# TensorE in written order through the whole program

## The chip, the core and the metric

The kernel runs on one core of a Trainium2 chip. The metric is the time of one execution in device microseconds; lower is better. TensorE (PE in the profile) does the matmuls and the transposes, VectorE (DVE) and ScalarE (ACT) the elementwise work, GpSimd (POOL) issues the indirect gathers, and SyncE (SP) the loads of the weights.

## The reference

A transformer-like net on 256 tokens of width 2048, in float32:

```python
# block 1
h = rmsnorm(x, g_norm1); proj = h @ w_in
y_a = mla_branch(proj, ...) @ w_o_mla        # latent attention, 8 heads, rope on 64 of 192 columns
y_b = diff_branch(proj, ...) @ w_o_diff      # softmax(q1 k1) - lam * softmax(q2 k2), 8 heads
gates = sigmoid(proj[..., OFF_GATE:] + b_gate)
x = x + (gates[..., :D] * y_a + gates[..., D:] * y_b) @ w_out
# peer: per token, 8 heads x 16 experts out of 16384, found by two top-16 searches
q = (h @ w_q).reshape(t, 8, 2, 128); s1, s2 = q . sub_keys
experts, gates = top16(top16(s1) + top16(s2))
a = gelu(sum_d expert_u[experts] * h)
x = x + sum_k (gates * a)[k] * expert_v[experts[k]];  x = rmsnorm(x, g_final)
# even mixer: 4 retention heads of 256 and a gated convolution of width 3, then w_out
x = x + even_mixer(rms_norm(x), ev_w_in, ev_conv_w, ev_w_out)
# odd mixer: 32 query heads on 4 key heads, a window of 128, sinks, a silu gate, then w_out
x = x + odd_mixer(rms_norm(x), od_w_in, ..., od_w_out)
```

## The kernel before

Every projection goes through `dense` (lines 158 to 186). A weight block of 512 columns (w_kr: 320) is loaded in parts of two k rows (line 106, SP); `prep` splits each part into a high half (ACT, line 109) and a low half (DVE, line 110), up to three parts ahead, in four buffers `hl`. PE then runs, for each k and each of the two token tiles (t0, t1), three matmuls into one PSUM bank: x_hi·w_hi (line 177), x_hi·w_lo (178), x_lo·w_hi (179). These are called dense matmuls below; the program has 6156 of them. The stages are block 1 (w_ckvq, w_kr, w_ukv, w_uq, w_dqkv, w_gate, then w_oa/w_ob, w_out), w_qp with the routing, the row stream, the even mixer (ev_in, ev_out) and the odd mixer (od_in, od_out).

After each part `dense` calls `tick`. When a block of columns is done, its two evacuations (`ev_...`, one for each t) are started as generators: each does its ACT and DVE work on the bank, yields a number of ticks, and then issues its transposes (`transpose4`, line 206) or score matmuls, which need the result of that work. Attention units (`mla_unit`, lines 471 to 482; `diff_unit`, 524 to 551; retention and the odd mixer's attention, 1115 to 1169) run as such generators between the parts too. `settle`, in the last k part of a projection's first block, and `flush`, called after some projections, tick until what is open is done; there all the rest is issued at once.

PSUM has four banks for `acc`, two for `tr` (transposes) and two for `sd` (scores and attention outputs).

In the row stream 256 groups of 128 gathered rows of expert_u and 256 of expert_v (128x2048 each) arrive by indirect DMA (line 773) in a few slots; DVE makes a dot product of each u group (line 799) and PE multiplies each v group (line 815). The first u gathers are issued, and their dots made, while w_qp still runs: `route` finds the experts of a block of heads (DVE, lines 653 to 703), writes them as `ef`, and `spread` transposes `ef` on PE (line 664).

What sets the order: the program is recorded through a tile framework whose scheduler orders the instructions of each engine by its own estimate of when their inputs are there. Only inside `with self.tc.manual_schedule(engines={PE, Pool})`, which before stands around the row stream's loop alone (line 846), do the named engines keep the order in which the code issues. DVE, ACT and POOL elsewhere, and PE elsewhere, are ordered by the scheduler.

Of the kernel before, what the change touches and what calls it, by code (L numbers as in the profile page):

```python
# [42 lines left out]
class Builder:  # L43
# [258 lines left out]
    def build(self):  # L302
        nc, d = self.nc, self.d
        for w in ("w_ckvq", "w_kr", "w_ukv", "w_uq", "w_dqkv", "w_gate", "w_oa", "w_out1", "w_qp"):
            if w == "w_oa":
                wa, wb = d["w_oa"], d["w_ob"]
                for b in range(4):
                    for ww in (wa, wb):
                        self.add_plan(ww[b:b + 1])
            else:  # L310
                self.add_plan(d[w])
        self.limit = len(self.plan)
        for w in ("ev_in", "ev_out", "od_in", "od_out"):
            self.add_plan(d[w])
        cst = self.cst
        self.mhalf = cst.tile([P, 8], F32, tag="mhalf", name="mhalf")
        nc.gpsimd.memset(self.mhalf, -0.5)
        self.ident = cst.tile([P, P], F32, tag="ident", name="ident")
        make_identity(nc, self.ident)
        wz = cst.tile([P, 512], F16, tag="wz", name="wz")  # L320
        nc.vector.memset(wz, 0.0)
        wp = self.sd()
        for _ in range(14):
            nc.tensor.matmul(wp, wz[:, :P], wz, start=True, stop=True)
        self.block1()
        self.peer()
        self.even()
        self.odd()

    def stat_sum(self, ss4, tag):  # L330
        out = self.cst.tile([P, 2], F32, tag=tag + "_ss", name=tag + "_ss")
# [954 lines left out]
```

## Time and profile before

| | |
|---|---|
| median of three runs | 2896.06 us (2892.47, 2896.06, 2896.06) |
| profiled execution | 2892.76 us, span 2891.0 us |
| PE busy | 2330.3 us, 81% |
| DVE busy | 1687.0 us, 58% |
| ACT busy | 790.2 us, 27% |
| POOL busy | 669.1 us, 23% |
| moved by DMA | 820.24 MB, 284 GB/s over the span |
| mean granted clock of PE | 0.898 |

The span runs from the first to the last instruction of the profiled execution; its time is a little longer. A share of busy time is a mean over stages with different limits, so the rows are read by stage. A number in brackets in a timeline row is the idle time of the engine ahead of it, and what ended it.

### The profile page before, as it was taken

How to read it: one execution, taken by the hardware profiler on the slowest of the kernel's cores; microseconds unless marked ns; L12 is line 12 of the kernel's file. 1: busy time of each engine (PE TensorE's matmuls, PEld its weight loads, DVE VectorE, ACT ScalarE, POOL GpSimd, SP SyncE). 2: the span in 40 equal slices, each digit the busy share in tenths (PEclk: the TensorE clock that was granted, in tenths of full speed). 3: DMA queues.
4: the chain of work that ended last, by engine and by line, in shares of the span. 5: the costliest groups of instructions: out<-in, count | busy, mean ns of one | idle time of the engine just before them, and what ended most of it. 6: DMA issues, size and time to landing. Idle time of an engine off the chain costs nothing.

```text
span 2891.0 us, 26312 instructions
## 1 busy us (share of the span) xinstructions
PE 2330.3 (81%) x9488; PEld 1460.5 (51%) x9488; DVE 1687.0 (58%) x2503; ACT 790.2 (27%) x1244; POOL 669.1 (23%) x570
## 2 busy tenths in 40 slices
PE   9999999999515656665666565667899999999999
PEld 7878888888401111111111111111488888888887
DVE  5665755667999554444455444441464556677754
ACT  6544644444200000000000000000344444456653
POOL 0000000000354564444445454533100000000000
PEclk9999999999857877778787868789999999999999
DMA  7545466556989999999999999999755455553345
GB/s 253 170 144 183 156 217 200 186 187 208 360 319 363 408 421 420 420 420 420 420 420 420 420 420 420 420 420 420 278 182 191 160 181 185 191 173 132 124 152 169
DMA packets 151955, 820.24 MB, mean 284 GB/s; under 512 B 17232, under 2 KB 17264, under 8 KB 85776
## 3 DMA queue, kind: packets, MB, share of 16 engines
q0 software_dynamic: 75360, 543.75, 46.0%
q1 hardware_dynamic: 76464, 274.81, 28.5%
q8 instruction: 74, 1.21, 0.2%
q14 instruction: 57, 0.47, 0.0%
HBM read 816.39 MB, written 2.10 MB: 283 GB/s over the span
## 4 chain that ended last, share of the span: by engine, by line
PE 52%; DMA 19%; issue 15%; POOL 8%; DVE 6%; ACT 0%; SPq 0%; POOLq 0%; ACTq 0%; DVEq 0%
PE acc L177 15%; PE acc L178 15%; PE acc L179 15%; DMA hg<-expert_v,eidv 7%; DMA gslot<-expert_v,eidv 7%; POOL gslot L773 4%; POOL hg L773 3%; DMA hj<-expert_v,eidv 2%; DVE hj L799 2%; PE tr L206 2%; PE acc L815 1%; DMA gslot<-expert_u,eidx 1%; PE sd L1115 1%; POOL hj L773 1%; PE sd L1124 1%
## 5 line engine op out<-in xcount | busy, mean ns | idle before, releaser
L110 DVE TENSOR_TENSOR hl<-raw,hl 128x1024 fp32r<-128x1024 f32 (+1 forms) x516 | 623.3, 1211 | 529.1 <-ACT hl L109 528.7
L109 ACT ACTIVATE hl<-raw 128x1024 fp32r<-128x1024 f32 (+1 forms) x516 | 541.2, 1049 | 766.8 <-PE acc L179 612.1
L177 PE MATMUL acc<-hl,h 128*128 128x512 f32 (+1 forms) x1472 | 582.4, 396 | 2.6 <-ACT hl L109 2.6
L178 PE MATMUL acc<-hl,h 128*128 128x512 f32 (+1 forms) x1472 | 573.8, 390 | 4.8 <-DVE hl L110 4.8
L815 PE MATMUL acc<-hg,lw 128*32 128x512 f32 x880 | 415.5, 823 | 199.7 <-DMA hg<-expert_v,eidv 195.8
L179 PE MATMUL acc<-hl,h 128*128 128x512 f32 (+1 forms) x1472 | 573.8, 390 | 0.0
L815 PE MATMUL acc<-gslot,lw 128*32 128x512 f32 x848 | 422.8, 820 | 174.0 <-DMA gslot<-expert_v,eidv 173.8
L799 DVE CUSTOM_DVE_ANT_0 hj<-gslot,hj 128x2048 f16<-128x2048 f32 x121 | 277.0, 2289 | 238.2 <-DMA gslot<-expert_u,eidx 238.1
L799 DVE CUSTOM_DVE_ANT_0 hj<-hg,hj 128x2048 f16<-128x2048 f32 x116 | 265.5, 2289 | 207.9 <-DMA hg<-expert_u,eidx 207.5
L177 PEld LDWEIGHTS acc<-hl,h 128*128 128x128 f32 x1472 | 277.6, 189 | 64.8 <-issue 6.6
L178 PEld LDWEIGHTS acc<-hl,h 128*128 128x128 f32 x1472 | 277.7, 189 | 61.5 <-DVE hl L110 7.2
L179 PEld LDWEIGHTS acc<-hl,h 128*128 128x128 f32 x1472 | 277.3, 188 | 57.6 <-issue 0.3
L815 PEld LDWEIGHTS acc<-hg,lw 128*32 128x32 f32 x880 | 81.1, 141 | 441.7 <-DMA hg<-expert_v,eidv 273.8
L815 PE MATMUL acc<-hj,lw 128*32 128x512 f32 x320 | 214.4, 825 | 88.1 <-DMA hj<-expert_v,eidv 88.1
L815 PEld LDWEIGHTS acc<-gslot,lw 128*32 128x32 f32 x848 | 81.7, 140 | 397.1 <-DMA gslot<-expert_v,eidv 252.4
L786 ACT ACTIVATE dots<-dots 128x32 f32<-128x32 f32 x8 | 1.8, 229 | 988.3 <-DVE dots L799 988.3
L194 POOL TENSOR_TENSOR rs_y<-rs_v,mhalf 128x2 f32<-128x2 f32 (+2 forms) x25 | 28.0, 1121 | 804.2 <-DVE rs_v L193 803.5
L773 POOL DMA_INDIRECT hg<-expert_v,eidv x110 | 147.6, 1342 | 181.6 <-PE acc L815 137.3
L773 POOL DMA_INDIRECT gslot<-expert_v,eidv x106 | 135.0, 1274 | 205.2 <-PE acc L815 164.8
L773 POOL DMA_INDIRECT gslot<-expert_u,eidx x121 | 129.2, 1068 | 179.4 <-issue 70.4
L773 POOL DMA_INDIRECT hg<-expert_u,eidx x116 | 139.7, 1204 | 118.9 <-issue 26.8
L815 PEld LDWEIGHTS acc<-hj,lw 128*32 128x32 f32 x320 | 40.8, 142 | 199.1 <-DMA hj<-expert_v,eidv 119.0
(303 smaller groups left out, 2393.8 us busy)
## 6 DMA issues: line engine op xcount, KB each, us to landing
raw<-ev_in SPq DMA_DIRECT2D x128, 512.0 KB, 4.5
raw<-od_in SPq DMA_DIRECT2D x72, 512.0 KB, 3.9
raw<-w_gate SPq DMA_DIRECT2D x64, 512.0 KB, 4.3
raw<-w_dqkv SPq DMA_DIRECT2D x48, 512.0 KB, 3.5
raw<-w_out SPq DMA_DIRECT2D x32, 512.0 KB, 3.9
raw<-w_qp SPq DMA_DIRECT2D x32, 512.0 KB, 4.4
raw<-ev_out SPq DMA_DIRECT2D x32, 512.0 KB, 4.6
raw<-od_out SPq DMA_DIRECT2D x32, 512.0 KB, 4.5
```

What stands on the lines that cost most here:

```text
L109: nc.scalar.activation(hi, raw, AF.Copy)
L110: nc.vector.tensor_tensor(lo, raw, hi.bitcast(F32), op=ALU.subtract)
L177: nc.tensor.matmul(o, xh, wh, start=(k == 0), stop=False)
L178: nc.tensor.matmul(o, xh, wl, start=False, stop=False)
L179: nc.tensor.matmul(o, xl, wh, start=False, stop=(k == kc * kk - 1))
L194: nc.gpsimd.tensor_tensor(y, v, self.mhalf[:, :n], op=ALU.pow)
L206: self.nc.tensor.transpose(ps[:, j * P:(j + 1) * P], row[:, j * P:(j + 1) * P], self.ident)
L773: nc.gpsimd.indirect_dma_start(out=g[0], out_offset=None, in_=d[table], in_offset=bass.IndirectOffsetOnAxis(ap=ix, axis=0))
L799: nc.vector.tensor_tensor_reduce(junk, g[0], hrow[:, t], 1.0, 0.0, op0=ALU.mult, op1=ALU.add, accum_out=dots[:, t, k:k + 1])
L815: nc.tensor.matmul(st["acc"][n][32 * q:32 * q + 32], lws[t, b][:, q, i], g[0][:, n * 512:(n + 1) * 512], start=(x % P < 4), stop=(x % P >= ...
L1115: nc.tensor.matmul(ps[:, i * W:(i + 1) * W], qT[hf, h // 2, q], kT[hf, g, :W], start=True, stop=True)
L1124: nc.tensor.matmul(po[:, i * 64:(i + 1) * 64], pT[:, i * (t + 1) + k], vo[:, k, g * 64:(g + 1) * 64], start=(k == 0), stop=(k == t))
```

## The change

The four stages are issued inside a `manual_schedule` for PE alone, so that PE's rows stand everywhere in the order in which the code issues them. The other engines are still ordered by the scheduler, whose rows move a little with PE's. The line numbers after 326 grow by one.

```diff
@@ -322,10 +322,11 @@
         wp = self.sd()
         for _ in range(14):
             nc.tensor.matmul(wp, wz[:, :P], wz, start=True, stop=True)
-        self.block1()
-        self.peer()
-        self.even()
-        self.odd()
+        with self.tc.manual_schedule(engines={mybir.EngineType.PE}):
+            self.block1()
+            self.peer()
+            self.even()
+            self.odd()
```

The first place is the end of w_kr on PE (`cl` are the latents that w_ukv multiplies, `ev` the rows that `ev_kr` made, `tr` the banks of transposes). Before, from the 7th dense matmul of w_ukv on:

```order
L177 MATMUL acc_717<-hl_624,cl_229 128x512
L178 MATMUL acc_717<-hl_624,cl_229 128x512
L206 MATMUL tr_726<-ident_84,ev_685 128x128 x2
L179 MATMUL acc_717<-hl_624,cl_229 128x512
L177 MATMUL acc_718<-hl_624,cl_229 128x512
L178 MATMUL acc_718<-hl_624,cl_229 128x512
L179 MATMUL acc_718<-hl_624,cl_229 128x512
L177 MATMUL acc_717<-hl_641,cl_229 128x512
L206 MATMUL tr_733<-ident_84,ev_677 128x128
L178 MATMUL acc_717<-hl_641,cl_229 128x512
L179 MATMUL acc_717<-hl_641,cl_229 128x512
L177 MATMUL acc_718<-hl_641,cl_229 128x512
```

And now, at the same place on PE (buffer numbers differ by a few):

```order
L178 MATMUL acc_520<-hl_609,h1_116 128x320
L179 MATMUL acc_520<-hl_609,h1_116 128x320
L206 MATMUL tr_721<-ident_84,ev_675 128x128 x2
L206 MATMUL tr_728<-ident_84,ev_687 128x128 x2
L206 MATMUL tr_735<-ident_84,ev_679 128x128
L206 MATMUL tr_738<-ident_84,ev_691 128x128
L177 MATMUL acc_719<-hl_626,cl_231 128x512
L178 MATMUL acc_719<-hl_626,cl_231 128x512
```

Of the four sets of transposes that stood behind the 1st, 8th, 13th and 16th dense matmul of w_ukv (the second and the third are in the rows of before) all now stand ahead of the first.

The second place is the end of ev_in on PE, where `flush` stands (`eT` is what ev_out multiplies). Before, from the 11th dense matmul of ev_out on:

```order
L178 MATMUL acc_11066<-hl_10988,eT_8399 128x512
L206 MATMUL tr_11047<-ident_84,ev_10895 128x128 x4
L179 MATMUL acc_11066<-hl_10988,eT_8399 128x512
L177 MATMUL acc_11065<-hl_11005,eT_8399 128x512
L178 MATMUL acc_11065<-hl_11005,eT_8399 128x512
L179 MATMUL acc_11065<-hl_11005,eT_8399 128x512
L177 MATMUL acc_11066<-hl_11005,eT_8399 128x512
L178 MATMUL acc_11066<-hl_11005,eT_8399 128x512
L179 MATMUL acc_11066<-hl_11005,eT_8399 128x512
L177 MATMUL acc_11065<-hl_11005,eT_8399 128x512
L206 MATMUL tr_11055<-ident_84,ev_10897 128x128 x4
```

And now there:

```order
L178 MATMUL acc_10902<-hl_10973,h3_7372 128x512
L179 MATMUL acc_10902<-hl_10973,h3_7372 128x512
L206 MATMUL tr_11049<-ident_84,ev_10897 128x128 x4
L206 MATMUL tr_11057<-ident_84,ev_10899 128x128 x4
L177 MATMUL acc_11067<-hl_10990,eT_8401 128x512
L178 MATMUL acc_11067<-hl_10990,eT_8401 128x512
```

The two sets of four transposes stood behind 11 and 19 dense matmuls of ev_out, and now stand ahead of the first.

The third place is the second route's spread in w_qp on PE (`ef` are expert numbers, `skT` the sub-keys, `at` a transposed query, `h2` the normed input). Before:

```order
L178 MATMUL acc_5754<-hl_5785,h2_4444 128x512
L664 MATMUL tr_5802<-ident_84,ef_5120 128x128
L206 MATMUL tr_5825<-ident_84,ev_5752 128x128 x4
L179 MATMUL acc_5754<-hl_5785,h2_4444 128x512
L177 MATMUL acc_5755<-hl_5785,h2_4444 128x512
L178 MATMUL acc_5755<-hl_5785,h2_4444 128x512
L179 MATMUL acc_5755<-hl_5785,h2_4444 128x512
L727 MATMUL sd_5857<-skT_5110,at_5830 128x128 x4
```

And now:

```order
L178 MATMUL acc_5757<-hl_5706,h2_4446 128x512
L179 MATMUL acc_5757<-hl_5706,h2_4446 128x512
L665 MATMUL tr_5804<-ident_84,ef_5122 128x128
L728 MATMUL sd_5814<-skT_5112,at_5783 128x128 x4
L206 MATMUL tr_5827<-ident_84,ev_5754 128x128 x4
L177 MATMUL acc_5756<-hl_5729,h2_4446 128x512
```

The spread moved 32 dense matmuls ahead, to before the scores of the third block's t0, which before stood 33 rows above it.

## Rows read from the trace of the kernel before

**Rows 1.** The page's slices: busy tenths in 40 equal slices.
```profile
PE   9999999999515656665666565667899999999999
DMA  7545466556989999999999999999755455553345
```

**Rows 2.** Busy time by stage: stretch, length, PE, PEld, DVE, ACT, POOL, PEclk, DMA, GB/s.
```profile
0.00:712.00 712.00, 706.57 (x3292) 578.62 (x3293) 445.24 (x631) 348.48 (x518) 16.27 (x31) 1.00 0.57 189
712.00:768.00 56.00, 50.04 (x235) 40.22 (x234) 50.68 (x130) 18.42 (x23) 16.78 (x13) 0.97 0.84 316
768.00:940.00 172.00, 54.79 (x142) 14.30 (x139) 169.56 (x436) 8.30 (x18) 86.22 (x57) 0.63 0.91 352
940.00:2063.00 1123.00, 696.85 (x1948) 150.28 (x1950) 503.05 (x462) 16.39 (x51) 523.16 (x443) 0.80 1.01 417
2063.00:2443.00 380.00, 379.76 (x1733) 312.87 (x1730) 229.83 (x316) 170.87 (x198) 8.08 (x13) 1.00 0.54 181
...
2543.00:2891.00 348.00, 342.29 (x1688) 281.25 (x1686) 225.14 (x451) 179.65 (x376) 16.22 (x10) 1.00 0.45 149
```

**Rows 3.** PE's waits, by what it waited for: us in total, times, longest.
```profile
PE tr L664 <- DVE ef L703: 64.3, 3, 32.9
...
PE acc L178 <- DVE hl L110: 4.8, 4, 1.8
```

**Rows 4.** Timeline of PE in w_ckvq: start us, us, engine, line, operation.
```profile
23.20 0.39 PE L177 MATMUL acc<-hl,h 128*128 128x512 f32 x1
...
23.88 0.39 PE L177 MATMUL acc<-hl,h 128*128 128x512 f32 x1
```

**Rows 5.** Timeline at the end of w_kr.
```profile
73.07 0.40 PE L177 MATMUL acc<-hl,cl 128*128 128x512 f32 x1
...
74.64 0.51 ACT L409 ACTIVATE ev<-acc,r 128x320 f32<-128x320 f32 x1
...
76.89 0.18 DVE L415 COPY ev<-ev 128x64 f32<-128x64 f32 x1
...
77.51 0.27 PE L206 MATMUL tr<-ident,ev 128*128 128x128 f32 x1
```

**Rows 6.** Timeline of a diff unit beside w_gate.
```profile
342.32 1.13 PE L524 MATMUL sd<-dqk 64*128 64x256 f32 x4
...
344.61 0.20 ACT L549 ACTIVATION_READ_ACCUMULATOR at<-sd 128x1 f32 x1
...
344.97 0.48 PE L524 MATMUL sd<-dqk 64*128 64x256 f32 x1
```

**Rows 7.** Timeline at the end of ev_in.
```profile
2441.75 0.74 DVE L1028 SCALAR_TENSOR_TENSOR ev<-acc,rr,ev 128x512 f32<-128x512 f32 x1
...
2442.64 0.63 PE L206 MATMUL tr<-ident,ev 128*128 128x128 f32 x4
...
2444.15 0.74 DVE L1028 SCALAR_TENSOR_TENSOR ev<-acc,rr,ev 128x512 f32<-128x512 f32 x1
...
2445.04 0.52 PE L206 MATMUL tr<-ident,ev 128*128 128x128 f32 x3
```

**Rows 8.** Timeline of w_qp, third and fourth block.
```profile
743.55 1.16 PE L727 MATMUL sd<-skT,at 128*128 128x128 f32 x8 [2.38 <-ACT at L723]
...
753.12 0.33 PE L664 MATMUL tr<-ident,ef 128*128 128x128 f32 x1 [1.08 <-DVE ef L703]
...
753.36 2.28 DVE L799 CUSTOM_DVE_ANT_0 hj<-gslot,hj 128x2048 f16<-128x2048 f32 x1
...
757.97 0.50 PE L178 MATMUL acc<-hl,h 128*128 128x512 f32 x1 [1.77 <-DVE hl L110]
```

**Rows 9.** Busy time in two stretches behind that wait, columns as in rows 2.
```profile
756.00:759.50 3.50, 1.73 (x8) 1.27 (x8) 3.40 (x10) 0.36 (x1) 2.42 (x2) 1.00 0.68 201
759.50:762.90 3.40, 3.40 (x10) 2.63 (x9) 3.40 (x12) 0.00 (x0) 0.81 (x1) 0.50 0.96 314
```

**Rows 10.** The page's group of the low halves: busy, mean ns, idle before.
```profile
L110 DVE TENSOR_TENSOR hl<-raw,hl 128x1024 fp32r<-128x1024 f32 (+1 forms) x516 | 623.3, 1211 | 529.1 <-ACT hl L109 528.7
```

## The prediction

> **What bounds the kernel now.** I read the page's slices first [rows 1]: PE is at 90% or more at both ends of the span, and in the middle, where PE sits near 60%, the DMA engines are full. The table by stage [rows 2] gives the borders. From 0 to 712 us (block 1) PE is busy 706.57 of 712 us, DMA 57%, DVE 63%: every microsecond in which PE stands there is added to the time. From 940 to 2063 (the row stream) DMA is full and PE waits for rows. From 2063 on (the two mixers) PE is busy again, 379.76 of 380 us and, in the last stretch, 342.29 of 348. Between lies the start of the stream: 712 to 768 (the queries' matmul, w_qp, beside the first routes), and 768 to 940, where DVE works 169.56 of 172 us.
>
> Then PE's waits [rows 3]: of those outside the stream's gathers the largest is for `ef` (64.3 us, of which all but 1.08 lie behind 753 us in the DVE-bound stretch); for low halves it waits 4.8 us in all. So in the stages that PE bounds it has almost no waits to lose: the scheduler has already put matmuls where a wait would stand.
>
> **The change part by part.** Nothing is added or removed; PE's rows change places, as the order shows. In before, where an evacuation's transposes or score matmuls come due, the scheduler lets some dense matmuls (lines 177 to 179) pass first, until its inputs should be there. In after they stand at the tick that issues them, and PE, which takes its queue in order, stands until the inputs come, with dense matmuls behind it whose inputs are ready. The wait that appears is about the work that no longer passes first: the number of dense matmuls times their spacing. The spacing is (23.88 - 23.20)/3 = 0.227 us, from two matmuls three places apart [rows 4].
>
> Counted in the order, block 1 has twelve such places: 16 matmuls at the end of w_kr; 3, 6, 5, 3 and 2 beside w_dqkv (the last rope of w_uq and the MLA units); 6, 7, 5, 6, 2 and 5 beside w_gate (the diff units): 66 in all. 66 x 0.227 = 15.0 us. Two places as a test of the method. At the end of w_kr the first matmul of w_ukv starts at 73.07; the second token tile's row is made from 74.64 on ACT, its rope's copy on DVE starts at 76.89 and takes 0.18, and the transpose that needs it ran at 77.51 [rows 5]. In written order the w_ukv matmul follows that transpose, so from about 77.1, some 4.0 us later; six transposes fill 0.9 of that (four take 0.63 [rows 7]), so PE stands 3.1 us, against 16 x 0.227 = 3.6 by the count. In a diff unit the first group of scores goes out at 342.32 and the second at 344.97, because its bank is free only when ACT has read it at 344.61 + 0.20 = 344.81 [rows 6]; without matmuls between, PE stands from 342.32 + 1.13 = 343.45 to 344.81, 1.36 us, against 6 x 0.227 = 1.36. So the count holds to within a seventh.
>
> The two mixers have 49 such matmuls (19 at the end of ev_in, 11 at the end of od_in, the other 19 in eight places of 1 to 4), and two places where a second transpose stood behind a pair of score matmuls, counted as two each: 53 x 0.227 = 12.0 us. The largest is the flush at the end of ev_in: both sets of transposes now stand ahead of ev_out's first matmul. In before the gate product of tile 0 ends on DVE at 2441.75 + 0.74 = 2442.49 and that of tile 1 at 2444.15 + 0.74 = 2444.89, each followed by its transpose 0.15 us later [rows 7]: PE now has to wait for the second, with nothing of its own.
>
> Bounds for these two terms: nothing, if DVE and ACT, whose rows the scheduler still orders and which in that stretch do casts ahead of the chain, finish the inputs as early as PE asks; and the count itself, 27.0 us, since PE ran without idling over those places in before. I take the count, because the two places tested come that near to it.
>
> Second cost, the clock. [...]
>
> Third, the start of the stream. The second route's spread (line 664) stands 32 dense matmuls earlier, ahead of the score matmuls of the next block. In before PE waits for `ef` 1.08 us at 753.12 [rows 8]. In DVE's new order the sum that makes `ef` comes behind two more dots of 2.28 us [rows 8] and one low half of 1.2 [rows 10], so at about 758.9; PE then has 32 x 0.227 = 7.3 us of matmuls more to do. So w_qp ends some 5.8 + 7.3 - 1.8 - 1.7 = 9.6 us later than 768 (the last two are the wait at 757.97 and its slow stretch, which go). What hides it: from 768 on PE is busy only 54.79 of 172 us, and DVE, which bounds the stretch, has the same dots to do and gets at two of them earlier. Queued behind the waiting transpose on PE are dense matmuls, the scores of the last two blocks, and through the casts' buffers four gathers on POOL. I cost it at 0.5 us, the excess that DVE's 169.56 of 172 leaves room for; bounds: 9.6 if DVE runs dry for that time, and -24.4 if the DMA engines' lulls all close (16% of 56 us and 9% of 172 [rows 2]).
>
> The stream itself was in written order already, and its PE rows are the same; DMA bounds it.
>
> Sum, against the profiled execution (span 2891.0, time 2892.76): 15.0 + 12.0 + 6.8 + 0.5 = 34.3, so 2927.1. Two of the three timed runs of before lie 3.3 us above that execution, one 0.3 below, so runs of after should lie from 2927 to 2930; I say 2928.
>
> **Rivals.**
> (a) The waits are half paid. For: DVE and ACT get other rows too, and without dense matmuls between, casts (line 110, 1211 ns each in DVE's queue [rows 10]) may move behind the chain that PE waits for. Against: most chains start with the block's last matmul, and their own length is what is waited for. 13.5 + 3.4 = 17 us: about 2911.
> (b) The delay of w_qp passes through to the stream, because DVE's 170 us of work start with the last block's scores. For: DVE has no slack there. Against: the dots that fill it need only rows, and the routes of the second tile come much later. 34.3 + 9.1: about 2937.
> [...]
> (d) The other side: the earlier second route gives the gathers earlier indices and closes the DMA lulls between 712 and 940. The stream's end moves forward by up to 24.4 us, and with a clock that doesn't fall the waits of 27.5 are all that stands against it: 2895.9, no change. It decides from 27.5 - 5.8 = 21.7 us, that is, if nine tenths of the lulls close. For: DMA is full from 940 on, so a row fetched earlier is time gained. Against: by the order two of the early gathers move behind four others, so as many are issued by 780 as before, and DVE, not the indices, holds the slots.
> That the change does nothing is ruled out by the order: the rows have moved.
>
> **How the numbers follow.** The forecast 0.62, (a) 0.14, (b) 0.08, (c) 0.09, (d) 0.07. A measurement tells 0.2% from no change, 5.8 us; all but (d) and the lower end of (a) lie beyond. Of (d) I give 0.02 to faster and 0.05 to the same, and 0.03 of (a) to the same: faster 0.02, same 0.08, slower 0.90. The forecast's own range is 2916 to 2934 (clock term 0 to 10, counts up to a quarter lower); for 8 in 10 it takes in the upper half of (a) and (b) and (c): 2908 to 2939.
>
> **What would show it.** In after's table of PE's waits, new entries for transposes (line 206) on ACT and DVE evacuations and for score matmuls (lines 471, 524) on the readers of their banks, 20 to 30 us together outside the stream; the wait for `ef` near 745 to 759 at 10 us or more. Block 1 should end some 15 to 20 us later, the stream last as long as now within 3 us, the mixers 12 to 16 us longer. Stretches at 0.50 behind some of the waits. I am wrong if block 1 ends at the same time: then the inputs came sooner than the count says; or if the stream's end moves by other than block 1's delay: then the w_qp term was mis-sized.

## The result and the profile after

The changed kernel takes 2936.19 us in the median of four runs (2935.38 to 2938.92), beside 2895.91 before: 40.3 us more, a ratio of 1.0145 (95% interval 1.0133 to 1.0157). The forecast was 2928 in a range of 2908 to 2939, slower. The profiled execution of after is its slowest run, 2938.92 us with a span of 2937.2, so between the two profiles the difference is 46.2 us; the stages below are read from these two, so they show some 6 us more than the medians do.

The starts of the same dense matmuls in the two timelines show where it came about (us; numbers are counts of dense matmuls):

| matmul | before | after | later by |
|---|---|---|---|
| first of w_ukv, behind w_kr (289th) | 73.07 | 78.24 | 5.17 |
| first of w_gate (1069th) | 284.21 | 301.55 | 17.33 |
| first behind w_gate (1837th) | 481.97 | 511.64 | 29.66 |
| first of w_qp (2605th) | 662.31 | 691.97 | 29.66 |
| last of w_qp (2988th) | 767.20 | 809.50 | 42.30 |
| first of ev_in (2989th) | 2066.68 | 2097.62 | 30.94 |
| first of ev_out (4525th) | 2440.10 | 2477.85 | 37.74 |
| last of od_out (6156th) | 2886.22 | 2932.40 | 46.18 |

Block 1 loses 29.7 us up to the end of w_gate and nothing from there to w_qp; w_qp loses 12.6, of which the stream gives back all but 1.3; the mixers lose 15.2. The table of PE's waits in after has the new entries (engine, line waited for, us in total, times, longest; `L665` is the line that was 664 before):

```profile
PE tr L665 <- DVE ef L704: 53.1, 2, 33.7
PE tr L665 <- DVE gate L715: 16.9, 1, 16.9
...
PE sd L525 <- DVE ev L552: 6.9, 4, 2.6
PE acc L178 <- DVE hl L110: 5.8, 5, 1.7
PE tr L206 <- DVE at L214: 4.3, 4, 2.8
PE tr L206 <- DVE ev L1029: 4.1, 2, 2.4
PE tr L206 <- DVE ev L247: 4.1, 3, 1.9
...
PE tr L206 <- DVE ev L1168: 2.3, 1, 2.3
PE tr L206 <- ACT at L285: 1.9, 4, 0.8
PE sd L525 <- DVE at L254: 1.9, 1, 1.9
```

Of the 4.3 us for `at` L214, 3.1 stood in before too, inside the row stream; of the other waits of lines 206 and 525 before had only 0.3 us (line 524, for L254). They are the places of the prediction, here in after's timeline (start us, us, the row, and in brackets the stand ahead of it):

```profile
76.17 0.44 PE L206 MATMUL tr<-ident,ev 128*128 128x128 f32 x2 [1.34 <-ACT ev L410]
...
77.39 0.33 PE L206 MATMUL tr<-ident,ev 128*128 128x128 f32 x1 [0.79 <-DVE at L214]
...
78.19 0.30 PE L206 MATMUL tr<-ident,ev 128*128 128x128 f32 x1 [0.47 <-DVE ev L416]
...
136.09 0.63 PE L206 MATMUL tr<-ident,ev 128*128 128x128 f32 x4 [1.88 <-DVE ev L247]
...
166.87 0.70 PE L472 MATMUL sd<-mla 128*128 128x256 f32 x2 [1.22 <-DVE oT L219]
...
180.07 0.66 PE L206 MATMUL tr<-ident,ev 128*128 128x128 f32 x4 [1.77 <-DVE ev L247]
...
307.43 2.52 PE L525 MATMUL sd<-dqk 64*128 64x256 f32 x8 [1.91 <-DVE at L254]
...
328.94 1.53 PE L525 MATMUL sd<-dqk 64*128 64x256 f32 x8 [1.66 <-DVE ev L552]
...
348.07 1.16 PE L525 MATMUL sd<-dqk 64*128 64x128 f32 x14 [1.49 <-DVE ev L552]
...
369.69 2.07 PE L525 MATMUL sd<-dqk 64*128 64x256 f32 x6 [2.56 <-DVE ev L552]
...
789.20 0.45 PE L665 MATMUL tr<-ident,ef 128*128 128x128 f32 x1 [16.86 <-DVE gate L715]
...
2474.71 0.63 PE L206 MATMUL tr<-ident,ev 128*128 128x128 f32 x4 [2.38 <-DVE ev L1029]
...
2477.11 1.09 PE L206 MATMUL tr<-ident,ev 128*128 128x128 f32 x4 [1.77 <-DVE ev L1029]
...
2842.86 1.23 PE L206 MATMUL tr<-ident,ev 128*128 128x128 f32 x8 [2.25 <-DVE ev L1168]
```

The first three answer to [rows 5], the two at 2474 and 2477 to [rows 7]. All such stands in block 1 (thirteen of 0.46 to 2.56 us between 76 and 392 us) add up to 17.6 us, those in the mixers (ten) to 10.6. The rest is the clock. Busy time in six stretches of after (length, PE, PEld, DVE, ACT, POOL, granted clock, DMA share, GB/s):

```profile
137.50:151.15 13.65, 13.65 (x37) 9.71 (x37) 4.39 (x9) 3.30 (x16) 0.00 (x0) 0.50 0.12 41
308.20:311.60 3.40, 3.40 (x10) 2.28 (x11) 3.25 (x7) 3.00 (x15) 0.00 (x0) 0.50 0.40 140
349.20:352.60 3.40, 3.40 (x9) 2.73 (x9) 3.16 (x9) 0.00 (x0) 0.07 (x1) 0.50 0.42 128
369.70:376.50 6.80, 6.80 (x17) 4.96 (x18) 4.75 (x13) 2.08 (x8) 1.03 (x1) 0.50 0.26 81
2475.70:2482.50 6.80, 5.39 (x15) 4.47 (x16) 3.84 (x6) 1.26 (x2) 1.64 (x3) 0.50 0.27 86
2844.30:2847.70 3.40, 3.40 (x10) 2.63 (x9) 1.35 (x3) 0.43 (x1) 0.00 (x0) 0.50 0.44 157
```

Each begins within 2 us of the end of one of the stands, and in each the granted clock is 0.50, half of the full clock. At half speed 27.25 us in block 1 cost 13.6, and 10.2 us in the mixers 5.1 (4.4 if the stand of 1.77 inside the fifth isn't counted twice). Stands and clock: 17.6 + 13.6 = 31.2 against the 29.7 of block 1, and 10.6 + 4.4 to 5.1 = 15.0 to 15.7 against the 15.2 of the mixers. The half is a little too much: at 0.50 after's dense matmuls start 0.427 us apart (at 148.22, 148.65 and 149.07) against 0.227, so a microsecond there costs 0.47, and 27.25 cost 12.8. What is left over is a balance of smaller terms that I did not draw up in full; among them are the start of the program (0.50 for 6.83 us at 8.58 in before, for 3.41 at 11.26 in after) and PE's waits for casts in w_ckvq (1.11 us in before, 2.17 in after).

The stages answer to [rows 2]; their borders are moved by the delays of the table, by 31 us and, at the end of w_qp, 42:

```profile
743.00:810.00 67.00, 49.49 (x234) 40.85 (x232) 61.82 (x148) 18.02 (x23) 19.71 (x15) 0.87 0.86 318
810.00:971.00 161.00, 51.23 (x142) 13.29 (x142) 160.41 (x421) 8.61 (x18) 82.66 (x54) 0.67 0.90 352
971.00:2094.00 1123.00, 696.58 (x1958) 150.29 (x1959) 502.75 (x462) 16.97 (x53) 523.49 (x443) 0.80 1.01 417
```

With these borders w_qp has 67 us instead of 56 and the DVE-bound stretch behind it 161 instead of 172, with DVE as full; the stream's 1123 us hold as much work of PE, DVE and POOL as before, at the same DMA share.

### The profile page after: what moved, and what is told of

Read it like the earlier page. It is cut to its first block, busy times and chain, and to the rows that moved or that the text cites. A ratio compares the mean times of both kernels' runs of the same rounds, so it can differ in the third digit from the quotient of the medians.

```text
span 2937.2 us, 26318 instructions
## 1 busy us (share of the span) xinstructions
PE 2339.8 (80%) x9488; PEld 1470.6 (50%) x9488; DVE 1689.5 (58%) x2503; ACT 790.1 (27%) x1244; POOL 669.3 (23%) x570
## 4 chain that ended last, share of the span: by engine, by line
PE 49%; DMA 19%; issue 15%; DVE 8%; POOL 7%; ACT 1%; SPq 0%; POOLq 0%; ACTq 0%; DVEq 0%
PE acc L177 15%; PE acc L178 14%; PE acc L179 14%; DMA hg<-expert_v,eidv 8%; DMA gslot<-expert_v,eidv 6%; DMA hj<-expert_v,eidv 4%; POOL gslot L774 3%; POOL hg L774 3%; DVE hj L800 2%; PE tr L206 1%; DVE hl L110 1%; PE sd L1116 1%; POOL hj L774 1%; DMA gslot<-expert_u,eidx 1%; PE acc L816 1%
## 5 line engine op out<-in xcount | busy, mean ns | idle before, releaser
L816 PE MATMUL acc<-gslot,lw 128*32 128x512 f32 x848 | 415.7, 802 | 172.6 <-DMA gslot<-expert_v,eidv 172.3
L194 POOL TENSOR_TENSOR rs_y<-rs_v,mhalf 128x2 f32<-128x2 f32 (+2 forms) x25 | 28.6, 1142 | 838.6 <-DVE rs_v L193 838.0
L774 POOL DMA_INDIRECT hg<-expert_u,eidx x116 | 146.2, 1261 | 124.8 <-DMA hg<-expert_v,eidv 33.4
```

Source lines behind the costliest of these rows:

```text
L194: nc.gpsimd.tensor_tensor(y, v, self.mhalf[:, :n], op=ALU.pow)
L774: nc.gpsimd.indirect_dma_start(out=g[0], out_offset=None, in_=d[table], in_offset=bass.IndirectOffsetOnAxis(ap=ix, axis=0))
L816: nc.tensor.matmul(st["acc"][n][32 * q:32 * q + 32], lws[t, b][:, q, i], g[0][:, n * 512:(n + 1) * 512], start=(x % P < 4), stop=(x % P >= ...
```

## The experiments

Each was timed beside runs of the kernel before on the same chip (medians 2893.75 us for e1 to e4, 2893.42 for e5 to e8, 2894.52 for e9 and e10, 2893.87 for e11); differences are against these.

**Which stage.** The written order is put around one stage at a time:

```diff
-        self.block1()
+        with self.tc.manual_schedule(engines={mybir.EngineType.PE}):
+            self.block1()
         self.peer()
         self.even()
```

This is e1 against the kernel before; in e2 the block stands around `even` and `odd`, in e3 around `peer`.

> PE in written order in block 1 alone; w_qp, the stream's start and the two mixers are ordered by the scheduler again. Theory (the time is lost in the stands of PE ahead of deferred transposes and scores, and in the clock that falls behind them, each stage for itself): block 1 loses what it lost in the changed kernel, 29.7 us there of which 17 are stands and 12 to 14 clock, the rest loses nothing: 2921 to 2926 us. Rival A (w_qp's 11 us of delay are what the stream passes on): about 2896 + 29.7 - 11 = 2915, since w_qp is as before. Rival B (the written order costs everywhere alike, through the order of the dense rows among themselves): a quarter to a third of the 40 us, by block 1's share of dense matmuls (2604 of 6156, 0.42): about 2913.

Measured: 2922.36 us (1.0096, 1.0081 to 1.0112), 28.6 more.

> PE in written order in the even and the odd mixer alone. Theory (stands and clock, each stage for itself): 15 us, of which 11 are stands and 3 to 5 clock: 2908 to 2911 us. Rival B (the order of the dense rows among themselves): 3168 of 6156 dense matmuls, 0.51 of 40 us: about 2917. If the mixers lose only what block 1 hands on to them, 2896.

Measured: 2910.05 us (1.0055, 1.0041 to 1.0069), 16.3 more.

> PE in written order in the routing stage alone (w_qp, and the row stream as before). Theory (w_qp ends 9 to 11 us later, and DVE's and the DMA engines' work in the stream's start hides all of it): 2893 to 2898 us, no change. Rival A (the delay is passed on to the stream): about 2907. Rival D (the earlier second route closes DMA lulls): 2880 or less.

Measured: 2892.41 us (0.9995, 0.9986 to 1.0004), no change. Its table of PE's waits has the same stand for `ef` in w_qp:

```profile
PE tr L665 <- DVE ef L704: 52.0, 2, 32.8
PE tr L665 <- DVE gate L715: 16.9, 1, 16.9
```

The three add up to 28.6 + 16.3 - 1.3 = 43.6, the whole change to 40.3. So each stage pays for itself, to within 3 us, and the 16.9 us for which PE stands in w_qp cost nothing that the times can tell. Rivals A, B and D of these expectations, with them (b) and (d) of the prediction, are out.

**The clock apart from the stands.** The changed kernel with matmuls of zeros that fill the stands at thirteen places (the expectation says eleven, its list has thirteen); one of them:

```diff
+    def warm(self, n):
+        ps = self.tr()
+        for _ in range(n):
+            self.nc.tensor.matmul(ps, self.wz[:, :P], self.wz, start=True, stop=True)
...
                 yield 2
+                if t == 1:
+                    self.warm(8)
                 to_T(rr, qrT, 4, t)
```

> The changed kernel, with matmuls of zeros (128x512, f16, about 0.22 us each at the full clock) put on PE at eleven of the places where it stood: 5 and 3 at the end of w_kr, 8 and 7 ahead of a rope's transposes, 5 ahead of an MLA unit, 8, 7, 6, 11 and 5 ahead of five diff units, 10, 7 and 9 at the ends of ev_in and od_in. They fill a stand and add nothing to the result; PE still can't go on before the inputs are there. Theory (behind the stands the clock falls, which costs 18 of the 40 us): the stretches at 0.50 behind these places go, the waits stay as filled time, 2921 to 2926 us. Rival C (the low stretches come from the rows themselves, small matmuls and transposes close together, and not from the stand): they stay, and the time stays at 2934 to 2939 or rises by what the fillers overshoot.

Measured: 2923.22 us (1.0101, 1.0086 to 1.0117), 29.5 more than before, where the changed kernel has 40.3. The part of block 1 with the stands, in after and here (columns as above):

```profile
60.00:420.00 360.00, 342.24 (x1609) 278.08 (x1609) 216.34 (x324) 169.12 (x303) 7.09 (x9) 0.96 0.48 157
```
```profile
60.00:420.00 360.00, 356.12 (x1726) 285.47 (x1725) 223.24 (x331) 173.53 (x307) 7.68 (x10) 1.00 0.50 165
```

The granted clock is 1.00 over the whole stretch, and behind the ends of ev_in and od_in the dense matmuls start 0.23 us apart (from 2466.49 and from 2830.30 on), as at the full clock. The fillers are as short as expected: nine of them take 2.12 us (at 2826.59). The first matmul behind w_gate starts 16.7 us later than before, not 29.7, and the mixers lose 11.1, not 15.2. PE can't go on any sooner; only what it does meanwhile is changed. So the written order costs 16.7 + 11.1 = 27.8 us with the clock full, and 10.8 us in the medians, 15.6 between the two spans (2937.2 and 2921.6), are the clock that fell behind the stands. Rival C is out.

**Written order with the rows issued later.** Four kernels take the stands away in the code, all or some of them, and leave the order written:

```diff
-        self.dense(d["w_kr"], h1, ev_kr)
+        self.dense(d["w_kr"], h1, ev_kr, urgent=False)   # settle doesn't wait for it
...
-                yield 2
+                yield 2 + t
                 to_T(rr, dqk[:, 4 * b:4 * b + 4], 4, t)
...
             def go():
+                yield 1
                 pss = [self.sd(), self.sd()]
...
-        self.dense(d["w_gate"], h1, ev_gate, rate=0.2)
+        self.dense(d["w_gate"], h1, ev_gate, rate=0.167)
...
         self.dense(d["ev_in"], h3, ev_in, rate=0.1)
-        self.flush()
```

This is e5, shortened, and the comment is mine. It also sets `rate=0.167` beside w_dqkv and the units' credit to zero behind it, settles w_kr's evacuation behind w_ukv (`self.flush("kr")`), and drops the flush behind od_in.

> PE in written order everywhere, as in the changed kernel, but the code issues the stalled rows later: the evacuation of w_kr doesn't have to be done before w_ukv, the second tile's rope transposes come one tick later, each MLA and diff unit starts one tick later and one in six ticks instead of five, and the flushes behind ev_in and od_in are gone (the next projection's last part settles what is open). Theory (the loss is where the rows stand, not that they are in written order): stands and low stretches go, 2893 to 2900 us, as before the change. Rival B (the order of the dense rows among themselves costs too): 2905 to 2915.

Measured: 2892.45 us (0.9997, 0.9988 to 1.0006): the whole loss is gone in sum, with all of PE's rows in written order. By stages, block 1 ends 4.7 us sooner than before the change, while the mixers still take 823.06 us instead of 819.54, with 3.9 us left in six stands. Of its waits only small ones are left outside the stream's start:

```profile
PE acc L178 <- DVE hl L110: 5.1, 5, 1.5
...
PE tr L208 <- DVE at L216: 3.1, 2, 2.8
PE acc L177 <- ACT hl L109: 2.6, 2, 2.0
PE tr L208 <- DVE ev L248: 1.3, 2, 0.7
```

The mixers' 3.5 us are covered by their six stands, so rival B, a cost of the dense rows' order among themselves, is out.

> The kernel with the later issue, and in w_qp the spread of the first tile's routes also issued five ticks later, with the gathers of expert_u free to go as soon as their indices are there. The 16.9 us that PE stood for it in w_qp should go, and w_qp end 10 us earlier. Theory (that delay is hidden by DVE's work in the stream's start): within 3 us of the kernel with the later issue. Rival A (the delay reaches the stream): 8 to 11 us less than that.

(The edit: `yield 5` ahead of the spread for the first tile, and the gathers of expert_u are let go when their indices are written, no longer behind the spread.) Measured: 2893.94 us (1.0000, 0.9991 to 1.0009). The last matmul of w_qp started at 763.63 instead of 774.55, 10.9 us sooner, and the first of ev_in at 2065.08 instead of 2064.06. The delay is hidden by the stream's start.

> The changed kernel with only the two flushes behind ev_in and od_in taken out. Theory (each place pays for itself: there PE stood 2.38, 1.77 and 2.25 us, and the clock was at 0.50 for 6.8 and 3.4 us behind them, which costs half of that, 5.1): 11 us less than the changed kernel, 2922 to 2928. With the stands alone and no clock: 2929 to 2931. Rival (the flush only moves the wait to the next settle): 2935 or more.

Measured: 2927.73 us (1.0113, 1.0098 to 1.0129), 34.3 more than before against 40.3, so 6.0 of the 11 us expected; the time alone doesn't part the theory from the stands without clock. The profile does. From the first matmul of ev_in to the last of od_out it loses 3.9 us instead of 15.2 in after, the 11 expected, and behind the ends of ev_in and od_in no stretch at 0.50 stands (the clock is 1.00 from 2475 to 2486 and from 2834 to 2846 too):

```profile
2476.00:2936.00 460.00, 443.99 (x2155) 365.82 (x2153) 290.34 (x534) 227.86 (x438) 18.66 (x14) 1.00 0.47 154
```

In this profile block 1, which is the changed kernel's, had 34 us at 0.50 instead of 27 and lost 3.0 us more; why the same rows meet a low clock for longer in one run than in another isn't shown. In e1, whose block 1 has the same rows and stands as after's, it fell at other places: not behind the stand of 1.88 us, which in after was followed by 13.65 us at 0.50, but behind that of 1.22, which in after left it full. The two stands in e1, and the stretches behind them (columns as above):

```profile
138.13 0.63 PE L206 MATMUL tr<-ident,ev 128*128 128x128 f32 x4 [1.88 <-DVE ev L247]
...
162.97 0.70 PE L472 MATMUL sd<-mla 128*128 128x256 f32 x2 [1.22 <-DVE oT L219]
```
```profile
138.20:151.80 13.60, 13.60 (x65) 10.54 (x66) 7.15 (x11) 5.07 (x18) 0.00 (x0) 1.00 0.17 54
165.19:168.60 3.41, 3.41 (x9) 2.31 (x8) 1.55 (x4) 1.09 (x4) 0.00 (x0) 0.50 0.04 13
```

> The changed kernel, where only the evacuation of w_kr need not be done before w_ukv. In the changed kernel PE stood there 1.34, 0.79 and 0.47 us, with the clock full behind it. Theory: 2 to 4 us less than the changed kernel, 2931 to 2934; a clock that falls at other places can hide that. The count of the prediction (16 dense matmuls, 3.6 us) says the same.

Measured: 2936.35 us (1.0140, 1.0121 to 1.0158), but its four runs lie between 2927.25 and 2941.28, so the time can't tell 3 us. In its profile the first matmul of w_ukv starts at 73.59, 0.5 us later than before and not 5.2, so the place itself is mended as expected; two later stretches at 0.50 were longer than in after's profile (6.8 and 3.4 us where 3.4 and none stood). Inconclusive in the time.

**A gain that no step of the prediction had.** In the kernel with the later issue (e5) block 1 ended 4.7 us sooner than before the change. Its score rows answer to [rows 6], where four records of one half took 1.13 us and four of the other came 2.65 us behind:

```profile
323.16 1.13 PE L531 MATMUL sd<-dqk 64*128 64x256 f32 x8
```

> PE in written order in block 1 alone, with the later issue there (w_kr's evacuation not awaited, ropes and units one tick later); everything behind block 1 is ordered by the scheduler, as before the change. In the kernel with the later issue everywhere block 1 ended 4.7 us sooner than before the change, though no row was taken out. Theory (the written order keeps the two score matmuls of a diff unit's pair next to each other, which use different 64-row halves of PE, eight of them taking 1.13 us; the scheduler had set the two halves apart, four and four of 1.13 us each, in four of six units): 2887 to 2891 us, 3 to 5 us less than before. Rival (the gain of block 1 is given back at the stream's start): 2892 to 2896.

Measured: 2888.47 us (0.9980, 0.9971 to 0.9989), 6.0 less than before: the fastest kernel of this study. Busy time of PE in the score matmuls alone (tile `dqk`; length, PE, granted clock, DMA share, GB/s), up to the end of w_gate, in before and here:

```profile
0.00:482.00 482.00, 11.24 (x64) 0.99 0.57 189
```
```profile
0.00:477.00 477.00, 6.86 (x64) 1.00 0.58 191
```

That is 4.4 us less, of the 5.1 by which block 1 ends sooner in this profile. The expectation's four of six units are not quite what before shows: in three the second half stands behind dense matmuls, and in two more it starts 0.6 and 0.4 us behind the first.

> The same kernel, but each diff unit issues the scores of its first half for all heads and then those of the second half, instead of the two halves by turns. Nothing else moves. Theory: eight matmuls take about 2.2 us instead of 1.13 in each of six units, so 5 to 7 us more than the kernel beside it. Rival (the halves have nothing to do with it, the gain came from the units' later start): the same time as the kernel beside it.

```diff
-                for i in range(nh):
-                    for m in range(2):
+                for m in range(2):
+                    for i in range(nh):
                         hf = slice(m * 64, m * 64 + 64)
```

Measured: 2890.34 us (0.9985, 0.9976 to 0.9994), 1.9 more than the one beside it and not 5 to 7, with intervals that overlap; the score matmuls are busy for 7.98 us instead of 6.86. The first row is of a unit on the first query tile, the second of one on the second; in the kernel beside it they take 1.16 and 1.13:

```profile
303.75 1.71 PE L531 MATMUL sd<-dqk 64*128 64x128 f32 x16
...
323.38 1.14 PE L531 MATMUL sd<-dqk 64*128 64x256 f32 x8
```

So the reason as I had put it, by turns, is wrong: where one half comes right behind the other, the eight of the second tile take 1.14 us, as by turns (1.13), while the sixteen of the first tile take 1.71, about halfway between the 1.16 by turns and the 2.32 of the two halves one by one (1.16 each in e11, at 306.67 and 310.70; two of the six units are on this tile). What is left as a guess is that nothing else may stand between them:

> The kernel with written order and later issue in block 1 alone, but each diff unit issues the scores of its second 64-row half one tick (12 dense matmuls) behind those of the first, and a unit starts in one of seven ticks instead of six. Theory (the halves run beside each other on PE when nothing of another kind stands between them; by turns or one after the other matters little): 1.13 to 1.16 us more in each of six units, so block 1 ends 5 to 7 us later than in the kernel without that tick, and the time is 2892 to 2896 us, as before the change. Rival (the gain came from the later start of the units): block 1 ends within 1 us of that kernel's, 2887 to 2890.

```diff
                 for m in range(2):
+                    if m:
+                        yield 1
                     for i in range(nh):
```

This is against e10; `rate` beside w_gate is 0.143.

Measured: 2896.39 us (1.0009, 1.0000 to 1.0018), 2.5 more than its runs of before where e9 has 6.0 less, so 8.6 apart; in the profiles block 1 ended 7.9 us later (first matmul behind w_gate at 484.75, not 476.83). Each half takes as long alone as both together in e9 (1.13 us, at 322.71):

```profile
329.76 1.13 PE L533 MATMUL sd<-dqk 64*128 64x256 f32 x4
334.21 1.13 PE L533 MATMUL sd<-dqk 64*128 64x256 f32 x4
```

Six units by 1.13 to 1.16 are 6.9 us, and the score matmuls are busy for 13.64 us instead of 6.86; the other 1 us of the profiles I did not trace.

## Why the prediction was right, and where it was off

*The stands.* The steps by counts, 15.0 us in block 1 and 12.0 in the mixers, measured 17.6 and 10.6 as stands, 16.7 and 11.1 as filled time (e4): 27.8 against 27.0. So the count of dense matmuls that had passed first gives the waits to come in sum. Place by place it is rougher, and that the sum comes so near is partly luck: w_kr was counted at 3.6 us, worked out at 3.1 and measured at 2.60, the places beside w_dqkv were counted at 4.3 and stood 6.1, and the smaller ones in the mixers came out shorter. The five longer diff units were put at 1.1 to 1.6 each; their stands were 1.22 to 2.56, four of them (6.9 us) waiting for DVE's copy out of the bank (`ev L552`), where the prediction's test had ACT's read.

*The clock: the step that was mis-sized.* No run shows the 6.8 us that the sum has for the clock: it was my estimate, four falls at 1.7 us each, which is half of the one stretch of 3.40 us at 0.50 in [rows 9]. What the runs showed in its place: six stretches that cost about 18 us in after's profile, and 10.8 us in the medians (e4). Of the six, three lasted twice or four times as long as that of [rows 9] (6.80, 6.80 and 13.65 us), the longest behind a stand of 1.88, shorter than the 2.38 of [rows 8] that cost nothing (in before the granted clock is 1.00 from 740 to 756 us). So I was short by 11 to 12 us on the profiles; on the medians, 40.3 against 34.3, it is 4 of the 6 us missed (the other 2 are e4's 29.5 against the 27.5 of the other terms). That is why block 1 ended 29.7 us later, outside the 15 to 20 given as a sign; the mixers' 15.2 lie in their 12 to 16. Which stand is followed by a slow clock differs from run to run (e1), so an estimate from the stands of before could not have told it. In e4, with zeros in the stands, the clock was 1.00 (60 to 420 us); in after it stayed at 0.50 for 13.65 us with PE busy throughout by its rows. What ends such a stretch isn't shown.

*The stream's start.* `ef` was put at 758.9, so at 788.6 with block 1's delay, and PE's stand at 10 us or more: it ended at 789.20 after 16.86. (The profile names the gate product, L715, as what ended it; the sum that makes `ef`, L704, ended 0.10 us ahead of that, at 789.06.) w_qp's end was put 9.6 us later (the 1.7 in that sum is half of the 3.40 us at 0.50 in [rows 9]), it came 12.6 later. The cost of 0.5 us was right as far as the times can tell: e3 and e6 measure no change. Rivals (b) and (d) failed there.

*Rival (a)*, half-paid waits, failed: with the clock full the written order costs 27.8 us in the two stages (e4), not 13.5.

*What I left out.* That before's order had cost something in itself: the scheduler had set the halves of the scores apart. In after little of that comes back, since in three units one pair of scores goes out and the rest stands for its bank: with the clock full the score matmuls are busy for 9.71 us (e4), against 11.24 before and 6.86 in e9. In e9 the time is 6.0 us less, of which the scores show 4.4.

## What to carry to other kernels

Where PE is the bound, count how many ready matmuls stand between a chain's end and its first consumer: in written order the sum of those numbers times their spacing is the wait to expect (here 27.0 us counted, 27.8 measured in e4). Issuing the consumer a tick later in the code bought it back here (e5, 2892.45 us beside 2893.42 before). Add to each stand the chance of a slow clock behind it, which here cost from a third to two thirds as much again as the stands themselves (10.8 us on 27.8 in the medians, about 18 on 28.2 in the profiles). A stand in a stage that another engine bounds can cost nothing: 16.9 us in w_qp changed no time here.

## What the runs showed of the hardware that I had not expected

- Behind a stand of 1.88 us the granted clock was at 0.50 for 13.65 us, though PE was busy all that time (13.65 of 13.65 us, 37 matmuls); behind stands of 1.22 and 1.77 us in the same kernel (at 166.87 and 180.07) it did not fall: it was 1.00 from 167 to 171 and from 180 to 186 us. In e1 the same stand of 1.88 was followed by the full clock, and that of 1.22 by 3.41 us at 0.50. So neither the length of the stand nor the rows around it decide alone.
- Score matmuls of a diff unit, whose two halves take rows 0 to 63 and 64 to 127 of their operands (`hf`): eight records of 64x256 take 1.13 us when the halves are neighbours in the queue (e9, at 322.71), and four of one half alone take 1.13 as well (e11, at 329.76 and 334.21).
